# A two-layer hybrid trunk on one core: earlier input loads, a stacked low-rank product, a variance in column groups, and three probability tiles

## The chip, the cores and the metric

The kernel runs on one core of one Trainium2 chip. The metric is the time of one execution in microseconds (us): the median of three runs before the change is 1816.46 us (1814.5 to 1818.36). TensorE (PE in the profile), VectorE (DVE), ScalarE (ACT) and GpSimd (POOL) each work through a queue of their own in order; SyncE (SP) only issues transfers, and ScalarE issues a few more.

## The reference

Input x has 1024 tokens of 1024 channels. Each of two layers does:

```
h    = rms_norm(x, g_pre);  proj = h @ w_in        # split among four mixers
NSA attention | chunked gMLP | Conformer convolution | RWKV-7 recurrence
x    = x + rms_norm(concat(branch * silu(gate)) @ w_out, g_post)
x    = x + sigmoid(x @ ple_gate) * (p[layer] @ ple_proj)
```

Four pieces matter here. RWKV needs two low-rank products per token, `tanh(wd) @ w_up` for the decay and `ad @ a_up` for the gate, each with 32 inputs and 256 outputs. The convolution branch ends in a layer norm over its 256 channels, so it needs one variance per token. Attention makes, per 128 queries, head and branch (selected blocks and window), a row of softmax probabilities over up to 1024 keys. And the embedding product `p @ ple_proj` needs nothing but p, which is an input.

## The kernel before, in words

The tokens are cut in two halves of 512 per layer; layer l and half h give four rounds. Data lie channel by token (128 channels by 512 tokens). A dense product in near-float32 precision is three passes of TensorE (L166, L167, L168) over high and low parts in the type float32r: high by high, high by low, low by high. `split_w` loads 128x512 weights into `ws`, ScalarE casts the high part to `wh` (L156), GpSimd subtracts to get the low part `wl` (L158), and in the first half of a layer the low part is stored for the second. Each product of plain float32, as those with `lu`, appears in the trace as two matmul instructions.

Each round runs steps in the order that a letter string in `ORDER` gives; the first round before is "XieHFBRNrGabscdnAAATCy". X loads eight tiles of x (tag `ab`), i loads p (two tiles of tag `ld`) and splits it into four tiles of tag `t2`, e is the embedding product (48 matmuls, written to memory as `ped`), H is the norm (squares summed into `qa`, L292 to L296; column sums on TensorE, L263; then scaling, L301, and splitting, L255 and L256, into `aT`). F is the front of RWKV: the projection of low-rank inputs and gates (LO), then for each of two channel pairs the projections of k, r and v, with the two low-rank products between (L387, L392). B (`setup_late`) writes zeros to the memory tables `Xd` that RWKV's solve (R) fills in part, and builds the attention's bias tables T and TC through a gather from memory (L131) and three products (L124, L135, L141). N is the attention's front, r the recurrence, G, T and C the convolution, A one attention tile of 128 queries, a, b, c, d the gates, s the gMLP.

The strings don't fix the order of instructions. A planner orders each engine's queue at build time: every instruction has its place in the program as priority, `high_priority(offset=n)` moves one ahead by n places, and whatever is ready in the planner's own simulated time goes first by priority. On the chip a queue is in order, so an instruction that the planner took for ready holds up what stands behind it. A tag has a fixed number of tiles (`BUFS`): `t2` has 7, `r4` (probabilities, and scratch of B) has 4, `ld` 5, the score banks `s` 2, the banks `mm` 2 and `c1` 1.

Pair j of F holds the `t2` tiles k, kk, sg, aa, cum and G at once, beside the low-rank inputs `lo`, which live until the last product of pair 1.

Of the kernel before, what the change touches and what calls it, by code (L numbers as in the profile page):

```python
# [8 lines left out]
F32 = mybir.dt.float32  # L9
F32R = mybir.dt.float32r  # L10
# [6 lines left out]
TH = 512  # L17
NT = 4
# [10 lines left out]
C_ID, C_MA, C_ML, C_SUM, C_FAR, C_HB, C_FLAG, C_HS, C_N = 0, 128, 320, 384, 416, 544, 672, 673, 675  # L29
S_ANTI, S_OH, S_N = 0, 128, 256  # L30
RROW = 2128
ORDER = ("XieHFBRNrGabscdnAAATCy",
         "HAFRNGrbsaAAAAdcniOexTgCy",
         "HFRNrGabscdniOxeAAgAATyC",
         "HFRNGraAbsAAnAcdOTxgCy")
# [6 lines left out]
class Trunk:  # L42
    def __init__(self, ctx, tc, a):
# [8 lines left out]
        self.low, self.keep = {}, True  # L52
        self.setup()

    BUFS = {"aT": 16, "ws": 3, "wh": 3, "wl": 3, "t2": 7, "y": 7, "rv": 2, "pt": 3, "r4": 4, "ab": 8,
            "smr": 6, "sma": 14, "smc": 8, "cv": 4, "ot": 3, "ld": 5, "qa": 1}
    PBUFS = {"mm": 2, "s": 2, "rp": 1, "pt": 1, "pv": 1, "c1": 1}

    def t(self, shape, tag, bufs=None, dt=F32):
        self.n += 1  # L60
        return self.sb.tile(shape, dt, tag=tag, bufs=bufs or self.BUFS[tag], name=f"{tag}_{self.n}")

# [40 lines left out]
        self.mix_dram = [self.dram.tile([D, TH], F32, name=f"mixd{i}") for i in range(2)]  # L103
        self.pe_dram = [self.dram.tile([D, TH], F32, name=f"ped{i}") for i in range(2)]

    def setup_late(self):
        nc, a = self.nc, self.a
        zz = self.t([128, 1024], "r4")
        nc.vector.memset(zz, 0.0)
        for i in range(2):  # L110
            for q in range(2):
                nc.sync.dma_start(self.Xd[i][:, q * 1024:q * 1024 + 1024], zz)

        rs = self.dram.tile([4, RROW], F32, name="rscratch")
        st = self.t([128, S_N], "r4")
        nc.sync.dma_start(st[:, :S_N], a["cst"][:, C_N:C_N + S_N])
        rb = self.const([32, 4], "rb")
        nc.sync.dma_start(rb, a["rel_bias"])
        row = self.t([128, 1024], "r4")
        row2 = self.t([128, 1024], "r4")  # L120
        nc.vector.memset(row[:4, :977], 0.0)
        nc.vector.memset(row2[:4, :1023], NEG)
        pr = self.ps("pt")
        nc.tensor.matmul(pr[:4, :128], rb, st[:32, S_OH:S_OH + 128], start=True, stop=True)  # L124
        mid = self.t([128, TH], "ld")[:4, :128]
        nc.vector.tensor_copy(mid, pr[:4, :128])
        nc.sync.dma_start(rs[:, :977], row[:4, :977])
        nc.sync.dma_start(rs[:, 977:1105], mid)
        nc.sync.dma_start(rs[:, 1105:2128], row2[:4, :1023])
        hk = self.t([128, 4, 257], "r4")  # L130
        nc.sync.dma_start(hk, bass.AP(tensor=rs.tensor, offset=rs.offset + 848,  # L131
                                      ap=[[1, 128], [RROW, 4], [1, 257]]))
        for p in range(2):
            pj = self.ps("pt")
            nc.tensor.matmul(pj, st[:, S_ANTI:S_ANTI + 128],  # L135
                             hk[:, 2 * p:2 * p + 2, 1:257], start=True, stop=True)
            nc.scalar.copy(self.T[:, 2 * p:2 * p + 2, :].rearrange("p a b -> p (a b)"), pj)
        nc.vector.memset(self.TC[:, :, :53], 0.0)
        nc.vector.memset(self.TC[:, :, 70:], NEG)
        pj = self.ps("pt")  # L140
        nc.tensor.matmul(pj[:, :68], st[:, S_ANTI:S_ANTI + 128], hk[:, :, 0:257:16], start=True, stop=True)  # L141
        nc.vector.tensor_copy(self.TC[:, :, 53:70], pj[:, :68].rearrange("p (a b) -> p a b", a=4))
# [165 lines left out]
    def layer_setup(self, l):  # L308
        nc, a = self.nc, self.a
        self.l = l  # L310
        par = self.par = self.t([128, P_N], "par", bufs=2)
        nc.sync.dma_start(par, a["par"][l])
        d = self.der = self.t([128, 16], "der", bufs=2)
        nc.vector.tensor_scalar(d[:, 0:7], par[:, P_MU:P_MU + 7], -1.0, 1.0, op0=OP.mult, op1=OP.add)
        nc.vector.tensor_scalar(d[:, 7:9], par[:, P_W0:P_W0 + 2], 0.5, None, op0=OP.mult)
        nc.vector.tensor_scalar(d[:, 9:11], par[:, P_A0:P_A0 + 2], 0.5, None, op0=OP.mult)
        nc.vector.tensor_scalar(d[:, 11:13], par[:, P_KA:P_KA + 2], -1.0, 1.0, op0=OP.mult, op1=OP.add)
        cw = self.cw = self.t([128, 72], "cw", bufs=2)
        nc.vector.tensor_scalar(cw[:, :62], par[:, P_CW:P_CW + 62], 0.5, None, op0=OP.mult)
        nc.vector.tensor_scalar(cw[:, 62:66], par[:, P_CLG:P_CLG + 4], 0.5, None, op0=OP.mult)  # L320
        nc.vector.tensor_scalar(cw[:, 66:70], par[:, P_CLG:P_CLG + 4], 0.25, None, op0=OP.mult)
        nc.vector.tensor_scalar(cw[:, 70:72], par[:, P_PWB:P_PWB + 2], 0.5, None, op0=OP.mult)
        lu = self.lu = self.t([64, 256], "lu", bufs=1)
        nc.sync.dma_start(lu[0:32], a["rwkv_w_up"][l])
        nc.sync.dma_start(lu[32:64], a["rwkv_a_up"][l])
        w2 = self.w2 = self.t([128, 2, 64], "w2", bufs=1)
        nc.sync.dma_start(w2, a["nsa_w2"][l].rearrange("e p d -> p e d"))
        self.halo = None
        self.xg = None
        self.KH, self.KL, self.VS = {}, {}, {}  # L330
        self.S = None
# [15 lines left out]
    def rwkv_front(self):  # L347
        nc = self.nc
        par, der = self.par, self.der
        self.halo_in = self.halo  # L350
        self.halo_out = self.halo = self.t([128, 8], "halo", bufs=2)
        lp = self.proj([(LO0, 64), (G0, 12)])
        lo = self.shift(lp, 64, 6)
        g = self.t2(TH)
        nc.scalar.copy(g[64:76], lp[64:76])
        pg = self.ps("rp")
        for t in range(NT):
            nc.tensor.transpose(pg[:, t * 12:t * 12 + 12], g[64:76, t * 128:t * 128 + 128], self.ident[64:76, 64:76])
        self.gate = self.t([128, NT, 12], "gate", bufs=2)
        gf = self.gate.rearrange("p a b -> p (a b)")  # L360
        nc.scalar.activation(gf, pg[:, :48], AF.Tanh, scale=0.5)
        nc.vector.tensor_scalar(gf, gf, 0.5, 0.5, op0=OP.mult, op1=OP.add)
        nc.scalar.activation(lo[0:32], lo[0:32], AF.Tanh)
        self.AR, self.BK, self.v, self.yT = [], [], [], []
        self.gc = self.t([128, 2, 8], "gc", bufs=2)
        for j in range(2):
            self.rwkv_pair(j, lo)

    def rwkv_pair(self, j, lo):
        nc = self.nc  # L370
        par, der = self.par, self.der
        js = slice(j * 128, j * 128 + 128)
        c3 = lambda x: x.rearrange("p (c j) -> p c j", j=64)
        k = self.shift(self.proj(K0 + j * 128), 128, 2 + j)
# [9 lines left out]
        nc.vector.tensor_scalar(rss, pss[:, :8], 1e-24, None, op0=OP.max)  # L384
        nc.vector.reciprocal(rss, rss)
        pw_ = self.ps("c1")
        nc.tensor.matmul(pw_, self.lu[0:32, js], lo[0:32], start=True, stop=True)  # L387
        sg = self.t2(TH)
        nc.scalar.activation(sg, pw_, AF.Tanh, scale=0.5, bias=der[:, 7 + j:8 + j])
        nc.vector.tensor_scalar(sg, sg, 0.5, 0.5, op0=OP.mult, op1=OP.add)  # L390
        pa = self.ps("c1")
        nc.tensor.matmul(pa, self.lu[32:64, js], lo[32:64], start=True, stop=True)  # L392
        aa = self.t2(TH)
        nc.scalar.activation(aa, pa, AF.Tanh, scale=0.5, bias=der[:, 9 + j:10 + j])
        nc.vector.tensor_scalar(aa, aa, 0.5, 0.5, op0=OP.mult, op1=OP.add)
# [17 lines left out]
        r = self.shift(self.proj(R0 + j * 128), 128, j, "y")  # L413
# [283 lines left out]
    def conv_out(self, par, cw, l, mixd, acc, z):  # L697
        nc = self.nc
        CT = "c1"
# [3 lines left out]
        pq = self.ps(CT)  # L703
        sqs = []
        for j in range(2):
# [1 line left out]
            sq = self.t([128, 544], "cv")[:, :TH]  # L707
            nc.scalar.activation(sq, acc[j], AF.Square)
            sqs.append(sq)
        for t in range(NT):  # L710
            for j in range(2):
                nc.tensor.matmul(pq[:, t:t + 1], sqs[j][:, t * 128:t * 128 + 128], self.ones[:, 0:1],
                                 start=(j == 0), stop=(j == 1))
        r = self.rstd(pq[:, :NT], NT, 1e-5, "smc")
        pr = self.ps(CT)
        for t in range(NT):
            nc.tensor.transpose(pr[:, t * 128:t * 128 + 128], r[:, t:t + 1].to_broadcast([128, 128]), self.ident)
# [333 lines left out]
    def load_split(self, src):  # L1051
        return self.split_cm(self.ld(src))

    def embed_in(self):
        nc, a, l, h = self.nc, self.a, self.l, self.h
        pT = []
        for k in range(2):
            x = self.ld(a["pT"][l, k * 128:k * 128 + 128, h * TH:h * TH + TH])
            hi, lo = self.t2(TH, F32R), self.t2(TH, F32R)
            nc.scalar.copy(hi, x)  # L1060
            nc.vector.tensor_sub(lo, x, hi.bitcast(F32))
            pT.append((hi, lo))
        return pT
# [119 lines left out]
    def run(self):  # L1183
        prev = conv = att = None
        for l in range(2):
            self.layer_setup(l)
            for h in range(2):
                self.h = h
                self.keep = h == 0
                mixd = self.mixd = self.mix_dram[h]  # L1190
                for step in ORDER[2 * l + h]:
                    if step == "A":
# [2 lines left out]
                        self.attention(att)  # L1195
                    elif step == "H":
                        self.hT = self.norm_T()
                    elif step == "B":
                        self.setup_late()
                    elif step == "F":  # L1200
# [3 lines left out]
                    elif step == "r":  # L1204
                        self.rwkv_steps()
                    elif step == "i":
                        pT = self.embed_in()
                    elif step == "e":
                        self.keep = False
                        self.embed_out(pT)  # L1210
                        self.keep = h == 0
                    elif step == "X":
                        with self.tc.high_priority():
                            self.xs = [self.load_x(k) for k in range(KT)]
                    elif step == "n":
                        self.rwkv_norm()
# [107 lines left out]
```

## Time and profile before

| | |
|---|---|
| median of three runs | 1816.46 us |
| profiled execution, its own time | 1819.83 us |
| its span | 1818.1 us |
| TensorE busy | 1687.8 us, 93% |
| VectorE / ScalarE / GpSimd busy | 66% / 44% / 22% |
| mean granted TensorE clock | 0.96 of full |
| DMA | 261 MB, 144 GB/s in the mean |

"Busy" counts the time from an instruction's start to its modelled end, so matmuls that follow one another overlap; the distance between their starts is what they cost. Idle time of TensorE before an instruction is listed with what ended it.

### The profile page before, as it was taken

What the parts mean: (1) busy time and instruction counts of PE and PEld (TensorE: products, weight loads), DVE (VectorE), ACT (ScalarE), POOL (GpSimd) and SP (SyncE); (2) the same over time, 40 slices, a digit from 0 to 9 for tenths busy, and PEclk for the clock granted to TensorE, in tenths of its full rate; (3) what the DMA queues carried; (4) which work ended last, traced back from release to release, by engine and by line L of the source; (5) the groups of instructions that cost most, each with busy time, mean ns of one, the idle gap of its engine ahead of it and who ended that gap; (6) DMA issues with size and microseconds to landing.
All of it is one profiled execution on the core that took longest, in us unless ns stands there. A gap on an engine that the chain in (4) does not pass through costs nothing. (4 is left out here: it accounts for less than half of the span.)

```text
span 1818.1 us, 29200 instructions
## 1 busy us (share of the span) xinstructions
PE 1687.8 (93%) x10068; PEld 1242.4 (68%) x10068; DVE 1208.3 (66%) x3217; ACT 797.0 (44%) x1801; POOL 402.8 (22%) x327
## 2 busy tenths in 40 slices
PE   4998899999999999988988989999999999998998
PEld 3676666667777767666666667766777777666777
DVE  3549997764988746756498971656568885464263
ACT  3432233554234655644322344545333446554453
POOL 2333333000011232223333323000000102323343
PEclk9999998899999999999998999999989999989999
DMA  8457544235854522574574455763475433114554
GB/s 263 127 154 177 157 148 119 76 95 130 214 154 128 167 93 87 171 211 116 137 179 138 141 180 175 237 177 93 124 190 152 130 99 112 43 51 140 173 167 123
DMA packets 361419, 261.19 MB, mean 144 GB/s; under 512 B 84652, under 2 KB 296624, under 8 KB 361272
## 3 DMA queue, kind: packets, MB, share of 16 engines
q1 hardware_dynamic: 318520, 245.17, 46.6%
q10 hardware_dynamic: 42752, 14.16, 3.1%
q8 instruction: 79, 1.29, 0.3%
q14 instruction: 68, 0.56, 0.1%
HBM read 191.50 MB, written 67.77 MB: 143 GB/s over the span
## 5 line engine op out<-in xcount | busy, mean ns | idle before, releaser
L166 PE MATMUL mm<-aT,wh 128*128 128x512 f32 (+1 forms) x1304 | 536.1, 413 | 6.1 <-DVE t L742 2.0
L167 PE MATMUL mm<-aT,wh 128*128 128x512 f32 (+1 forms) x1304 | 531.3, 408 | 3.9 <-DVE aT L256 3.9
L168 PE MATMUL mm<-aT,wl 128*128 128x512 f32 (+1 forms) x1304 | 530.2, 407 | 0.2 <-POOL wl L158 0.2
L158 POOL TENSOR_TENSOR wl<-ws,wh 128x512 fp32r<-128x512 f32 (+1 forms) x228 | 308.8, 1356 | 704.3 <-ACT wh L156 596.5
L156 ACT CAST wh<-ws 128x512 fp32r<-128x512 f32 (+2 forms) x388 | 236.9, 611 | 484.7 <-PE mm L167 301.6
L166 PEld LDWEIGHTS mm<-aT,wh 128*128 128x128 f32 (+1 forms) x1304 | 249.6, 192 | 66.7 <-issue 6.0
L167 PEld LDWEIGHTS mm<-aT,wh 128*128 128x128 f32 (+1 forms) x1304 | 249.4, 191 | 58.5 <-DVE aT L256 7.6
L168 PEld LDWEIGHTS mm<-aT,wl 128*128 128x128 f32 (+1 forms) x1304 | 249.3, 191 | 51.7 <-issue 3.8
L692 DVE SCALAR_TENSOR_TENSOR cv<-cv,cw,cv 128x512 f32<-128x512 f32 x240 | 200.3, 850 | 2.3
L1030 ACT ACTIVATE r<-s,sma 128x512 f32<-128x512 f32 (+3 forms) x192 | 105.7, 554 | 51.3 <-DVE sma L1028 48.0
L606 POOL TENSOR_TENSOR q<-SB,gc 128x256 f32<-128x256 f32 x28 | 22.7, 811 | 476.3 <-DVE SB L619 178.8
L971 ACT COPY pt<-pt 128x512 f32<-128x512 f32 (+1 forms) x152 | 80.5, 530 | 104.2 <-PE pt L968 103.5
L968 PE MATMUL pt<-cst,r 128*128 128x128 f32 x528 | 103.3, 294 | 7.4 <-DVE r L1035 7.2
L976 PEld LDWEIGHTS pv<-pt,vs 128*64 128x64 f32 x1056 | 56.6, 138 | 59.3 <-ACT pt L971 47.3
L976 PE MATMUL pv<-pt,vs 128*64 128x128 f32 x1056 | 95.1, 292 | 1.7 <-ACT pt L971 1.0
L968 PEld LDWEIGHTS pt<-cst,r 128*128 128x128 f32 x528 | 60.9, 143 | 45.5 <-issue 26.7
L1020 DVE CUSTOM_DVE_ANT_0 s<-s,T 128x256 f32<-128x256 f32 (+1 forms) x144 | 54.1, 379 | 44.5 <-PE s L1001 43.5
L1000 PE MATMUL s<-kv,qs 128*128 128x512 f32 (+2 forms) x192 | 74.5, 390 | 2.0 <-ACT r L1030 1.9
L1035 DVE TENSOR_SCALAR r<-r,sma 128x640 f32<-128x640 f32 (+7 forms) x128 | 68.1, 532 | 1.0
L1001 PE MATMUL s<-kv,qs 128*128 128x512 f32 (+2 forms) x192 | 65.8, 347 | 0.0
L1032 DVE TENSOR_TENSOR sma<-sma 128x1 f32<-128x1 f32 x64 | 14.8, 231 | 71.3 <-ACT r L1030 71.0
L1110 DVE SCALAR_TENSOR_TENSOR ot<-ot,ld 128x512 f32<-128x512 f32 x24 | 25.1, 1048 | 50.3 <-ACT ot L1109 45.3
(328 smaller groups left out, 2666.5 us busy)
## 6 DMA issues: line engine op xcount, KB each, us to landing
ws<-in_w_in_dram SPq DMA_DIRECT2D x232, 256.0 KB, 3.2
wl<-low SPq DMA_DIRECT2D x156, 256.0 KB, 2.8
low<-wl SPq DMA_DIRECT2D x140, 256.0 KB, 2.1
ws<-in_ple_gate_dram SPq DMA_DIRECT2D x64, 256.0 KB, 3.1
ws<-in_w_out_dram SPq DMA_DIRECT2D x60, 256.0 KB, 2.9
ped<-ot ACTq DMA_DIRECT2D x32, 256.0 KB, 3.8
ld<-in_nsa_w_dram SPq DMA_DIRECT2D x32, 256.0 KB, 4.1
ld<-ped SPq DMA_DIRECT2D x32, 256.0 KB, 4.0
```

Of the source, the lines that this page charges most:

```text
L156: nc.scalar.copy(hi[:, :cols], st[:, :cols])
L158: nc.gpsimd.tensor_sub(lo[:, :cols], st[:, :cols], hi[:, :cols].bitcast(F32))
L166: nc.tensor.matmul(out, lh, rh, start=first, stop=False, skip_group_check=shared)
L167: nc.tensor.matmul(out, lh, rl, start=False, stop=False, skip_group_check=shared)
L168: nc.tensor.matmul(out, ll, rh, start=False, stop=last, skip_group_check=shared)
L692: nc.vector.scalar_tensor_tensor(ac, xg[j][:, k:k + TH], cw[:, j * 31 + k:j * 31 + k + 1], ac, op0=OP.mult, op1=OP.add)
L968: nc.tensor.transpose(pt[:, o:o + 128], P[e][:, (b + x - b0) * 128:(b + x - b0) * 128 + 128], self.ident)
L971: nc.scalar.copy(PT[:, :n], pt[:, :n])
L976: nc.tensor.matmul(acc[e], w.VS[hh][:, tt, br], PT[:, o:o + 128], start=False, stop=br == 1 and b + x == i, skip_group_check=True)
L1000: nc.tensor.matmul(p[:, :n], w.QS[hd][:, qs], w.KH[br, hh][:, c0 * 128:c1 * 128], start=True, stop=False)
L1030: nc.scalar.activation(P[:, o:o + wd], p[:, c:c + wd], AF.Exp, bias=ng[:, 0:1], accum_out=den[:, x:x + 1])
L1035: nc.vector.tensor_scalar(P[:, :n], P[:, :n], r, None, op0=OP.mult)
```

## The change

The first transfers: X and, in the first round, the two loads of p get an offset of 20000, ahead of the weights' 4000. `setup_late` is cut in two: the zeros for `Xd` become a step Z at its old place, and the rest (B) goes behind the gate a. The low-rank weights become one 128-row stack: high parts in rows 0 to 63, low parts in rows 64 to 127, for both products side by side; the inputs become two stacks LW and LA, so that one float32r pass of 128 rows gives what two float32 instructions over 32 rows gave. The convolution's variance has the ones as the stationary operand, four groups of 32 columns, and a transpose back. `r4` has three tiles.

```diff
-ORDER = ("XieHFBRNrGabscdnAAATCy",
+ORDER = ("XieHFZRNrGaBbscdnAAATCy",
-    BUFS = {... "r4": 4, ...}
+    BUFS = {... "r4": 3, ...}
+    def zero_tables(self):      # step Z: the memset of zz and the four stores to Xd, out of setup_late
...
-        lu = self.lu = self.t([64, 256], "lu", bufs=1)
-        nc.sync.dma_start(lu[0:32], a["rwkv_w_up"][l])
-        nc.sync.dma_start(lu[32:64], a["rwkv_a_up"][l])
+        st = self.t([128, TH], "ld")
+        for i, nm in enumerate(("rwkv_w_up", "rwkv_a_up")):
+            for r in range(4):
+                nc.sync.dma_start(st[32 * r:32 * r + 32, i * 256:i * 256 + 256], a[nm][l])
+        lu = self.lu = self.t([128, TH], "lu", bufs=1, dt=F32R)
+        nc.scalar.copy(lu, st)
+        nc.vector.tensor_sub(lu[64:128], st[64:128], lu[64:128].bitcast(F32))
...
+        LW, LA = self.t2(TH, F32R), self.t2(TH, F32R)
+        for x, hi, lw in ((LW, slice(0, 32), slice(32, 64)), (LA, slice(32, 64), slice(0, 32))):
+            nc.scalar.copy(x[hi], lo[hi])
+            nc.vector.tensor_sub(x[lw], lo[hi], x[hi].bitcast(F32))
+            nc.scalar.copy(x[64:128], x[0:64].bitcast(F32))
...
-        nc.tensor.matmul(pw_, self.lu[0:32, js], lo[0:32], start=True, stop=True)
+        nc.tensor.matmul(pw_, self.lu[:, js], LW, start=True, stop=True)
-        nc.tensor.matmul(pa, self.lu[32:64, js], lo[32:64], start=True, stop=True)
+        nc.tensor.matmul(pa, self.lu[:, 256 + j * 128:384 + j * 128], LA, start=True, stop=True)
...
-        for t in range(NT):
-            for j in range(2):
-                nc.tensor.matmul(pq[:, t:t + 1], sqs[j][:, t * 128:t * 128 + 128], self.ones[:, 0:1],
+        for j in range(2):
+            for t in range(NT):
+                nc.tensor.matmul(pq[32 * t:32 * t + 32, 0:128], self.ones[:, 0:32], sqs[j][:, t * 128:t * 128 + 128],
                                  start=(j == 0), stop=(j == 1))
-        r = self.rstd(pq[:, :NT], NT, 1e-5, "smc")
+        vr = self.t([128, 544], "cv")[:, :128]
+        nc.scalar.copy(vr, pq[:, 0:128])
+        pq = self.ps(CT)
+        nc.tensor.transpose(pq[:, 0:128], vr, self.ident)
+        r = self.rstd(pq[:, 0:128].rearrange("p (t i) -> p t i", t=NT)[:, :, 0], NT, 1e-5, "smc")
...
-    def embed_in(self):
+    def embed_in(self, first=0):
-            x = self.ld(a["pT"][l, k * 128:k * 128 + 128, h * TH:h * TH + TH])
+            with self.tc.high_priority(offset=first):
+                x = self.ld(a["pT"][l, k * 128:k * 128 + 128, h * TH:h * TH + TH])
-                        pT = self.embed_in()
+                        pT = self.embed_in(20000 if l + h == 0 else 0)
-                        with self.tc.high_priority():
+                        with self.tc.high_priority(offset=20000):
```

## Rows read from the trace of the kernel before

**Rows 1.** Page, part 1: engine, busy us, share, instructions.
```profile
PE 1687.8 (93%) x10068; PEld 1242.4 (68%) x10068; DVE 1208.3 (66%) x3217; ACT 797.0 (44%) x1801; POOL 402.8 (22%) x327
```

**Rows 2.** Waits of PE: line, releaser, total us, times, longest us.
```profile
PE mm L166 <- ACT t L1060: 18.9, 1, 18.9
...
PE pt L135 <- DMA r<-rscratch: 6.2, 1, 6.2
```

**Rows 3.** Windows: length, busy us of PE, PEld, DVE, ACT, POOL, clock, DMA, GB/s.
```profile
9.00:15.00 6.00, 0.00 (x0) 0.00 (x0) 0.00 (x0) 0.00 (x0) 0.00 (x0) 1.00 1.04 286
...
18.87:33.60 14.73, 14.73 (x53) 11.18 (x53) 8.57 (x20) 9.88 (x19) 3.75 (x3) 1.00 0.84 293
33.60:43.70 10.10, 2.50 (x14) 1.66 (x14) 4.77 (x8) 2.75 (x5) 2.25 (x2) 0.74 0.95 226
...
58.80:99.90 41.10, 39.77 (x190) 28.33 (x188) 26.33 (x56) 18.65 (x32) 16.42 (x11) 1.00 0.48 140
150.00:300.00 150.00, 133.04 (x936) 98.22 (x935) 138.95 (x318) 50.68 (x121) 53.75 (x43) 0.94 0.54 152
```

**Rows 4.** Timeline of the start: start us, us, engine, line, operation, count [idle before].
```profile
3.67 0.62 ACT L156 CAST wh<-ws 128x512 fp32r<-128x512 f32 x1 [1.59 <-DMA ws<-in_ple_proj_dram]
...
13.88 0.43 SPq L324 DMA_DIRECT2D lu<-in_rwkv_w_up_dram  x1
...
15.28 0.94 SPq L1048 DMA_DIRECT2D ld<-in_pT_dram  x2
...
18.20 0.62 ACT L1060 CAST t<-ld 128x512 fp32r<-128x512 f32 x1 [9.95 <-DMA ld<-in_pT_dram]
...
19.75 2.88 ACT L295 ACTIVATE t<-ab 128x512 f32<-128x512 f32 x5
```

**Rows 5.** Timeline of the norm's pace and of TensorE behind it.
```profile
39.01 0.68 DVE L256 TENSOR_TENSOR aT<-ab,aT 128x512 fp32r<-128x512 f32 x1
39.61 0.75 DVE L301 SCALAR_TENSOR_TENSOR ab<-ab,par,qa 128x512 f32<-128x512 f32 x1
...
42.61 2.07 PE L135 MATMUL pt<-r,r 128*128 128x512 f32 x2 [6.25 <-DMA r<-rscratch]
```

**Rows 6.** Timeline of PE around the decay's product of pair 1.
```profile
82.08 0.39 PE L167 MATMUL mm<-aT,wh 128*128 128x512 f32 x1
82.31 0.39 PE L168 MATMUL mm<-aT,wl 128*128 128x512 f32 x1
82.63 1.12 PE L387 MATMUL c<-t,lu 32*128 32x512 f32 x2
83.68 0.50 PE L166 MATMUL mm<-aT,wh 128*128 128x512 f32 x1
```

**Rows 7.** Timeline of DVE in F: pair 0's tile G, then pair 1's k.
```profile
66.25 0.07 DVE L399 MEMSET t<- 128x8 f32 x1
...
75.22 0.74 DVE L423 SCALAR_TENSOR_TENSOR y<-y,par,t 128x512 f32<-128x512 f32 x1
...
83.79 0.75 DVE L339 SCALAR_TENSOR_TENSOR t<-mm,par,t 128x511 f32<-128x511 f32 x1 [5.81 <-ACT t L338]
```

**Rows 8.** Timeline of PE: products in four column groups, and a convolution variance.
```profile
138.89 1.30 PE L869 MATMUL pt<-ld,t 128*32 128x128 f32 x40
...
1610.36 2.11 PE L712 MATMUL c<-ones,cv 128*128 128x1 f32 x16
1612.34 0.88 PE L968 MATMUL pt<-cst,r 128*128 128x128 f32 x3
```

**Rows 9.** Timeline: exponentials, and transposes that read the tile three before.
```profile
371.81 0.44 PE L968 MATMUL pt<-cst,r 128*128 128x128 f32 x2
371.90 0.57 ACT L1030 ACTIVATE r<-s,sma 128x384 f32<-128x384 f32 x1
...
1631.68 0.37 ACT L1030 ACTIVATE r<-s,sma 128x128 f32<-128x128 f32 x1 [0.17 <-DVE sma L1028]
...
1632.34 0.66 PE L968 MATMUL pt<-cst,r 128*128 128x128 f32 x4
```

More of the change, by code (lines that the diff above doesn't have):

```diff
@@ L53, in __init__ @@
         self.setup()
-    BUFS = {"aT": 16, "ws": 3, "wh": 3, "wl": 3, "t2": 7, "y": 7, "rv": 2, "pt": 3, "r4": 4, "ab": 8,
+    BUFS = {"aT": 16, "ws": 3, "wh": 3, "wl": 3, "t2": 7, "y": 7, "rv": 2, "pt": 3, "r4": 3, "ab": 8,
             "smr": 6, "sma": 14, "smc": 8, "cv": 4, "ot": 3, "ld": 5, "qa": 1}
@@ L104, in setup @@
         self.pe_dram = [self.dram.tile([D, TH], F32, name=f"ped{i}") for i in range(2)]
-    def setup_late(self):
-        nc, a = self.nc, self.a
+    def zero_tables(self):
+        nc = self.nc
         zz = self.t([128, 1024], "r4")
@@ L112, in setup_late @@
                 nc.sync.dma_start(self.Xd[i][:, q * 1024:q * 1024 + 1024], zz)
+    def setup_late(self):
+        nc, a = self.nc, self.a
         rs = self.dram.tile([4, RROW], F32, name="rscratch")
@@ L366, in rwkv_front, with rwkv_pair @@
         for j in range(2):
-            self.rwkv_pair(j, lo)
-    def rwkv_pair(self, j, lo):
+            self.rwkv_pair(j, LW, LA)
+    def rwkv_pair(self, j, LW, LA):
         nc = self.nc
@@ L1197, in run @@
                         self.hT = self.norm_T()
+                    elif step == "Z":
+                        self.zero_tables()
                     elif step == "B":
```

## The prediction

> **What bounds the kernel now.** I read the page's busy shares first, then what TensorE waited for, then the stretches, then the order of the first 60 us. TensorE is busy for 1687.8 us, 93% of the span [rows 1], so a saving counts where it takes work from TensorE while that is the engine others wait for, or removes one of its few long waits. The list of waits shows where those are: of some 130 us idle (span less busy time), one piece of 18.9 us is the start, before the first product, and one of 6.2 us is the wait of L135 for the gathered bias table [rows 2]. In the stretches the reader is to see three kinds of time. From 18.87 to 33.6 TensorE does the embedding product e without a gap; from 33.6 to 43.7 it does 2.5 us of work in 10.1 us at a clock of 0.74; in F, from 58.8 to 99.9, it is busy for 39.8 of 41.1 us [rows 3]. And from 150 to 300 VectorE is busy for 139 of 150 us, TensorE for 133: there VectorE and the recurrence's chain set the pace [rows 3].
>
> **The start.** Before, the two p loads are issued at 15.28, behind weights, constants, parameters and all of x, and the first cast of p runs at 18.20 [rows 4]. ScalarE has done one square of x by then; the next five come at 19.75, only after p's split has taken its `t2` tiles, which suggests that a tag's tiles go out in program order [rows 4]. After the change x and p are issued first, then weights. Ahead of the first product lie ten loads and one of weights, 11 x 256 KB = 2.88 MB; at the 286 GB/s of the saturated start [rows 3] that is 10.1 us. The first load of before, issued at 0.81 us, could be cast at 3.67 [rows 4], of which its own 0.9 us are in the sum, so some 2 us come on top of 0.8: p and weights are there at 12.9, and after a cast of 0.62 TensorE starts at 13.5 instead of 18.87, 5.4 earlier. If program order of the tag `ld` forced the eight small low-rank loads ahead of p, 8 x 0.43 of issue [rows 4] would take 3.4 of this back.
>
> The embedding product then runs from 13.5 to 28.2 (14.7 us, as now). Behind it, the norm: now TensorE starts F's products 10.1 us after e ended. 6.2 of these are L135, which stands ahead of F in TensorE's queue; the first `aT` pair was complete at 39.69 [rows 5], 6.1 us after e. With B gone from here F starts at 28.2 + 6.1 = 34.3. VectorE makes a pair in 0.75 + 0.69 = 1.44 us [rows 5], eight pairs end 10.1 us after the first, and the last pair's six products take 1.4: the first 48 products of F end at 45.8, where they end at 58.8 now. That is 13.0 us. Upper bound: with x there at 11 us the norm runs beside e and F starts right behind it; 48 x 0.23 [rows 6] from 28.2 end at 39.2, 19.6 us gained. Lower bound: 13.0 - 3.4 = 9.6. I take 13.0, since squares and casts stand in ScalarE's queue beside e's evacuations now as well.
>
> **B moved.** L135's first pair (2.07 us at the low clock, now in idle time [rows 5]) moves between dense work: half of it, 1.0, at full clock, and some 0.4 for the small products of L124, so +1.4. SP is passed by B's six transfers, which stood among the first weights. The wait for the gather can return: 0 to 6.2. It has dense work of a and b around it, so I take 0. Z keeps four stores of 512 KB, 7 us at 286 GB/s, beside F, which has DMA at a share of 0.48 [rows 3]: nothing; without that cover up to 3 us in weights.
>
> **The low-rank products.** The decay's product of pair 1 starts 0.32 us after the dense pass before it, where passes follow at 0.23, and the next dense pass 1.05 later [rows 6]. One float32r pass costs 0.23 in its place: at least 1.05 - 0.23 = 0.82 each, with the entry 0.91; 16 of them give 13 to 14.6 us of TensorE time. Added per round: four ScalarE copies and two subtractions of up to 0.62 and 0.69 (4 x 0.62 + 2 x 0.69 = 3.9 us), beside the dense products of k. What of the 13 us is a gain? LW and LA are two tiles of the seven where `lo` was one. Pair 0 with both is eight tiles, so its G must wait until LW is free, that is for pair 1's decay product. TensorE takes it by priority after r, v and k of dense work: now G comes at 66.25 and that product at 82.63 [rows 6, 7]. So pair 0's chain (66.25 to 75.96 [rows 7]) shifts to about 83 less what F got shorter, and pair 1's k, evacuated at 83.79 now [rows 7], waits for a tile of it. I put F's chain at the same end as now, with TensorE some 4 us ahead of it. Rounds 1 and 3 (the first halves), which VectorE and the chain pace [rows 3], then gain nothing from the product and pay two subtractions, +1.4 each; the other two keep 2 x 3.4 = 6.8. Bounds: 14.6 gained in all; or a loss, a rival below. The layer's `lu` split (one copy, one subtraction, twice) and six more issues of 0.43 on SP lie under other loads.
>
> **The variance.** 16 instructions take 1.98 us now [rows 8]; in four column groups 40 take 1.30, so 16 take 0.52 [rows 8], and the transpose 0.3, a third of 0.88: 1.2 us less of TensorE, four times. But the chain gets longer by a copy, under the 0.62 of a 512-column cast [rows 4], and the transpose, 0.9 at most. Bounds -4.8 to +3.6; I take -1.5, nearer to the TensorE row, as convolutions run beside attention.
>
> By the Trainium skill, "TensorEngine Tiling (Array Packing)", Key Properties, changing the tiling mode drains TensorE. The trace agrees with 0.32 - 0.23 = 0.09 us at the entry to the 32-row product [rows 6]. By this rule the new groups pay 2 x 0.09 four times, 0.7, and sixteen entries of 32-row products vanish, 1.4; without the rule both are zero. It changes the sum by less than a microsecond.
>
> **Three probability tiles.** I paired each of the 128 branches' exponentials with the transposes that read the tile three branches before, since with three tiles the one must wait for the other. In 12 of the 128 the exponential starts before these transposes end, first at 371.90 (end 372.1 by the modelled ends), last at 1631.68, while transposes of 1632.34 still read [rows 9]; these overlaps add up to 12.9 us. The other 116 already keep three tiles' distance, as the two banks `s` are the closer limit. What queues behind a late exponential is ScalarE's next copy `pt`, and TensorE's transposes; dense passes stand between. Bounds 0 to 13; I take 3.
>
> **Sum**, against the profiled execution's own 1819.83 us: -13.0 + 1.4 - 6.8 + 2.8 - 1.5 + 3 = -14.1, so 1805.7. The median lies 3.4 us under that execution (1816.46), so the prediction is 1802. Its own range, with half of the open bounds either way, is 1793 to 1811.
>
> **Rivals.**
> Fuller gain: the norm runs beside e (-19.6) and TensorE's saved passes count nearly in full (-11), B +1.4, variance -3, tiles +1: -31; halfway between that and the forecast, 1793. For it: TensorE at 93%. Against: ScalarE's order at the start. Chance 0.18.
> Lost on the way: the start gives 9.6, B's gather costs 3 of its 6.2, low-rank products 3, and the +1.4, +2.8 and +3 stay: -2.4, 1814. For it: the VectorE-bound stretches and a planner that doesn't know real landings. Chance 0.11.
> Three tiles bind: all 12.9 instead of 3, in attention where TensorE has idle waits for softmax: -4.2, 1812. Chance 0.08.
> The other side, the eighth `t2` tile: if the pair chains run one behind the other, F's chain ends 9.7 us later in each of four rounds, 39 us, and nothing of the 6.8 stays. With the start this is -13.0 + 1.4 + 39 + 2.8 - 1.5 + 3 = +32 at worst; with TensorE filling two of the four rounds, about +12: 1828. It decides once TensorE is idle for over 6 us per round beside F and the solve behind it. For it: the count of tiles. Against: dense work of N that is ready there. Chance 0.09.
> Transfers that don't lead: if p stays behind, the start gains only what B leaves, 6 us: 1809, within the forecast's range. Chance 0.05. The forecast itself has 0.49.
>
> **Numbers.** 0.2%, 3.6 us, is about what can be told from no change. Faster takes the forecast (0.48), the fuller gain (0.18), the transfers that don't lead (0.05) and half the third, 0.75; slower the eighth tile and a piece of the second, 0.13; same 0.12. The range 1785 to 1818 leaves out the eighth tile and the far ends.
>
> **What would show it.** Right: the first L166 near 13.5, F's first 48 products ended near 46, no wait of L135 before F; L387 and L392 at 0.23 each; G of pair 0 behind pair 1's L387; four quick groups in L712's place; ScalarE waits for L968 a little more often. Wrong: a first product later than 17, TensorE idle beside F or before L538, the gather's wait back at 6 us, or attention tiles over 1 us longer each.

## The result, and the profile after: 1.35% slower

The changed kernel takes 1841.55 us in the median of four runs (1836.29 to 1841.92), the kernel before beside it 1815.49: a ratio of 1.0135, interval 1.0117 to 1.0152. The forecast was 1802, with 1785 to 1818 as its range. The profiled execution has a span of 1839.5 us (own time 1841.4), 21.4 more than before. Lines are shifted: the dense passes are L168, L169 and L170, the low-rank products L398 and L403, G's memset L410, the column groups of attention L884.

The page's first part, columns as in [rows 1]:

```profile
PE 1682.2 (91%) x10056; PEld 1236.3 (67%) x10056; DVE 1212.2 (66%) x3227; ACT 810.3 (44%) x1823; POOL 393.8 (21%) x327
```

TensorE has less to do than before (1682.2 for 1687.8) and the span is longer: its idle time has grown by 27 us, to 157. The list of TensorE's waits (line, releaser, total, times, longest) answers [rows 2]; the last line is of the kernel before, where the column groups are L869:

```profile
PE pt L884 <- DMA ld<-in_nsa_w_dram: 33.5, 12, 9.7
PE mm L168 <- ACT t L1076: 20.7, 1, 20.7
...
PE mm L265 <- DVE qa L298: 4.9, 1, 4.9
...
PE pt L869 <- DMA ld<-in_nsa_w_dram: 15.9, 9, 4.3
```

The start has grown from 18.9 to 20.7, L135's wait is gone and L265's stands in its place, and the attention's column groups wait 33.5 us for weights (15.9 before). The windows answer [rows 3], for the embedding product, the norm, F, and 150 to 300 with its first third:

```profile
20.66:35.40 14.74, 14.06 (x48) 10.58 (x48) 6.12 (x9) 9.70 (x18) 2.99 (x3) 1.00 0.82 285
35.40:46.00 10.60, 2.88 (x12) 2.39 (x13) 3.34 (x6) 2.85 (x6) 2.29 (x2) 0.71 1.00 315
59.90:109.00 49.10, 43.64 (x200) 33.64 (x200) 27.02 (x57) 21.37 (x36) 15.27 (x12) 0.90 0.45 131
...
150.00:300.00 150.00, 129.59 (x910) 93.99 (x909) 134.16 (x317) 49.00 (x117) 45.45 (x40) 0.90 0.55 150
150.00:200.00 50.00, 34.82 (x169) 25.41 (x168) 47.17 (x91) 9.94 (x21) 15.62 (x11) 0.83 0.59 144
```

F and its products took 41.1 us and take 49.1, at a clock of 0.90 instead of 1.00. From 150 to 300 TensorE is busy for 129.6 us (133.0 before); most of the idle time lies in the first third. Why the start is late stands in the timeline of SP and ScalarE [rows 4]:

```profile
16.50 0.49 SPq L328 DMA_DIRECT2D ld<-in_rwkv_w_up_dram  x1
17.04 0.89 SPq L1063 DMA_DIRECT2D ld<-in_pT_dram  x2
17.98 1.35 SPq L328 DMA_DIRECT2D ld<-in_rwkv_w_up_dram  x3
...
19.99 0.62 ACT L1076 CAST t<-ld 128x512 fp32r<-128x512 f32 x1 [6.78 <-DMA ld<-in_pT_dram]
```

p is issued right behind the first of the low-rank staging loads, at 17.04 (15.28 before), though its offset is 20000. Both take tiles of the tag `ld`, and the staging tile comes first in the program. The norm follows the embedding product as late as before: its column sums stand at 39.66, F's products at 46.00 [rows 5].

```profile
39.66 1.76 PE L265 MATMUL mm<-onec,qa 128*128 128x1 f32 x8 [4.93 <-DVE qa L298]
...
46.00 1.13 PE L168 MATMUL mm<-aT,wh 128*76 128x512 f32 x2 [2.11 <-ACT aT L257]
```

In F, the timelines of PE [rows 6] and of DVE [rows 7]:

```profile
82.75 0.40 PE L170 MATMUL mm<-aT,wl 128*128 128x512 f32 x1
82.98 0.39 PE L398 MATMUL c<-t,lu 128*128 128x512 f32 x1
83.21 0.40 PE L168 MATMUL mm<-aT,wh 128*128 128x512 f32 x1
```

```profile
69.82 1.23 DVE L408 TENSOR_TENSOR_SCAN t<-scanm,t 128x512 f32<-128x512 bf16 x1
...
83.45 0.07 DVE L410 MEMSET t<- 128x8 f32 x1 [3.84 <-PE c L398]
...
90.80 1.75 DVE L434 SCALAR_TENSOR_TENSOR y<-y,par,t 128x512 f32<-128x512 f32 x1
```

A low-rank product costs 0.23, as dense passes do. Pair 0's decays are summed by 71 us (the scan, L408), and its G comes at 83.45, released by pair 1's L398: the eighth tile. The chain behind it ends at 92.6 instead of 75.96 [rows 7]. It is so in every round: from the start of pair 0's scan to its G the four rounds take 13.6, 26.1, 13.6 and 25.1 us, where they took 1.2 to 2.5 before, and each time G follows pair 1's L398 by 0.4 to 0.6.

### The profile page after: what moved, and what is told of

Its sections match the earlier page's. It is cut to its first block, busy times and chain, and to the rows that moved or that the text cites. A ratio compares the mean times of both kernels' runs of the same rounds, so it can differ in the third digit from the quotient of the medians.

```text
span 1839.5 us, 29256 instructions
## 1 busy us (share of the span) xinstructions
PE 1682.2 (91%) x10056; PEld 1236.3 (67%) x10056; DVE 1212.2 (66%) x3227; ACT 810.3 (44%) x1823; POOL 393.8 (21%) x327
## 3 DMA queue, kind: packets, MB, share of 16 engines
q1 hardware_dynamic: 319096, 245.57, 45.8%
## 5 line engine op out<-in xcount | busy, mean ns | idle before, releaser
L168 PE MATMUL mm<-aT,wh 128*128 128x512 f32 (+1 forms) x1304 | 540.9, 417 | 11.8 <-DVE y L668 4.2
L169 PE MATMUL mm<-aT,wh 128*128 128x512 f32 (+1 forms) x1304 | 533.5, 410 | 3.6 <-DVE aT L258 3.5
L170 PE MATMUL mm<-aT,wl 128*128 128x512 f32 (+1 forms) x1304 | 532.9, 409 | 0.0
L160 POOL TENSOR_TENSOR wl<-ws,wh 128x512 fp32r<-128x512 f32 (+1 forms) x228 | 301.5, 1325 | 699.1 <-ACT wh L158 590.4
L168 PEld LDWEIGHTS mm<-aT,wh 128*128 128x128 f32 (+1 forms) x1304 | 250.8, 193 | 74.4 <-ACT aT L257 6.9
L169 PEld LDWEIGHTS mm<-aT,wh 128*128 128x128 f32 (+1 forms) x1304 | 250.8, 192 | 58.2 <-DVE aT L258 7.5
L170 PEld LDWEIGHTS mm<-aT,wl 128*128 128x128 f32 (+1 forms) x1304 | 250.3, 192 | 52.5 <-issue 2.5
L703 DVE SCALAR_TENSOR_TENSOR cv<-cv,cw,cv 128x512 f32<-128x512 f32 x240 | 195.8, 835 | 2.2
L617 POOL TENSOR_TENSOR q<-SB,gc 128x256 f32<-128x256 f32 x28 | 21.4, 763 | 499.4 <-DVE SB L630 206.2
L258 DVE TENSOR_TENSOR aT<-ab,aT 128x512 fp32r<-128x512 f32 x64 | 51.0, 801 | 6.4 <-ACT aT L257 6.1
```

Of the source, the lines that this page charges most:

```text
L160: nc.gpsimd.tensor_sub(lo[:, :cols], st[:, :cols], hi[:, :cols].bitcast(F32))
L168: nc.tensor.matmul(out, lh, rh, start=first, stop=False, skip_group_check=shared)
L169: nc.tensor.matmul(out, lh, rl, start=False, stop=False, skip_group_check=shared)
L170: nc.tensor.matmul(out, ll, rh, start=False, stop=last, skip_group_check=shared)
L703: nc.vector.scalar_tensor_tensor(ac, xg[j][:, k:k + TH], cw[:, j * 31 + k:j * 31 + k + 1], ac, op0=OP.mult, op1=OP.add)
```

## The experiments

Each was timed beside the kernel before, whose medians in the four groups of kernels were 1816.0 to 1816.8 (1747 to 1749 at full clock). A kernel has four or ten timed runs, and they spread by 4 to 22 us; the interval is that of the ratio, so two medians that differ by a few us are often not clear of noise. A second number helps to read them: the span times its mean granted clock, in the median of all timed runs of a kernel, is what TensorE's clock offered, in microseconds at 2.4 GHz ("at full clock" below). The rest of the span is what the 1.2 GHz level left out. It is a split and not a price, for a stretch that waits on another engine at the low level loses nothing by it.

| kernel | median us | ratio to before, interval | at full clock | left out |
|---|---|---|---|---|
| before (beside the last group, 31 runs) | 1816.5 | | 1747 | 67 |
| after | 1841.6 | 1.0135 [1.0117, 1.0152] | 1759 | 81 |
| no_stack | 1803.1 | 0.9919 [0.9888, 0.995] | 1740 | 60 |
| stack_only | 1845.4 | 1.0153 [1.0118, 1.0189] | 1756 | 88 |
| t2_eight | 1811.9 | 0.998 [0.9959, 1.0] | 1742 | 68 |
| decay_early | 1811.4 | 0.9972 [0.9952, 0.9992] | 1747 | 63 |
| stage_in_pt | 1825.5 | 1.0045 [1.0025, 1.0064] | 1754 | 69 |
| eight_and_pt | 1806.8 | 0.9941 [0.992, 0.9962] | 1732 | 73 |
| eight_no_stack | 1810.3 | 0.9974 [0.9954, 0.9994] | 1746 | 62 |
| no_stack_eight | 1800.0 | 0.9922 [0.9895, 0.9948] | 1742 | 55 |
| one_pass | 1802.4 | 0.9927 [0.9903, 0.9951] | 1736 | 65 |
| three_p_tiles | 1814.7 | 0.9985 [0.9969, 1.0002] | 1746 | 68 |
| start_only | 1809.2 | 0.9961 [0.9942, 0.9979] | 1740 | 69 |
| variance_only | 1829.4 | 1.0065 [1.0042, 1.0088] | 1753 | 73 |
| start_three | 1806.6 | 0.9941 [0.992, 0.9961] | 1741 | 63 |
| mended_old_variance | 1820.2 | 1.0031 [1.0005, 1.0057] | 1733 | 86 |
| variance_three | 1823.2 | 1.0028 [1.0004, 1.0053] | 1753 | 68 |
| variance_moved | 1813.2 | 0.9986 [0.9962, 1.0009] | 1749 | 62 |

### Which part costs it

**no_stack**: the change without the stack.

```diff
-        lu = self.lu = self.t([128, TH], "lu", bufs=1, dt=F32R)     # and st, LW, LA and their copies
+        lu = self.lu = self.t([64, 256], "lu", bufs=1)
-        nc.tensor.matmul(pw_, self.lu[:, js], LW, start=True, stop=True)
+        nc.tensor.matmul(pw_, self.lu[0:32, js], lo[0:32], start=True, stop=True)
```

> The changed kernel without the stacked low-rank product: lu, its two loads and the four-pass products as before; early loads, moved tables, column-group variance and three probability tiles stay. If the stack is the whole loss (by the tile it needs and by its staging tile ahead of p): 1803 to 1810, as then the start's gain of 10 us is left. If the other three edits cost time as well: 1815 or more.

**stack_only**: the kernel before with the stack and with three probability tiles.

```diff
-    "r4": 4
+    "r4": 3
-        nc.tensor.matmul(pw_, self.lu[0:32, js], lo[0:32], start=True, stop=True)
+        nc.tensor.matmul(pw_, self.lu[:, js], LW, start=True, stop=True)     # with st, lu, LW and LA as in the change
```

> The kernel before with the stacked low-rank product and three probability tiles alone (with four there is no room for the stack's tiles). If the stack is the loss: 1835 to 1845, F's chain ends about 10 us later in every round. If the loss comes of the moved tables or the variance: within 5 us of 1816.

The stack is the whole loss: without it 1803.1, 38.5 under the change; with nothing else but the three tiles 1845.4, 29 over before (three tiles alone cost nothing, see below). All the rest of the change together gains 14. The two figures for the stack need not be equal: in the change its staging tile also holds p up, which the section on the start prices.

### What in the stack costs it

**t2_eight** gives the change one more tile of the tag.

```diff
-    "t2": 7
+    "t2": 8
```

> The changed kernel with eight t2 tiles in place of seven, nothing else. Theory 1 (the eighth tile: pair 0's G waits for pair 1's decay product, each round's F chain ends about 10 us later): G of pair 0 comes within 5 us of its scan again, F's chain ends some 9 us earlier in each round, and the time falls by 20 us or more, to 1821 or less. Rival (the loss is the start, where p's loads were held behind the low-rank staging tile): this changes nothing at the start, the time stays within 5 us of 1841.

**decay_early** keeps seven tiles and moves one product: pair 1's L398 goes ahead, so that LW is read for the last time before pair 0 wants its G.

```diff
-        pw_ = self.ps("c1")
-        nc.tensor.matmul(pw_, self.lu[:, js], LW, start=True, stop=True)
+        with self.tc.high_priority(offset=1000 * j):
+            pw_ = self.ps("c1")
+            nc.tensor.matmul(pw_, self.lu[:, js], LW, start=True, stop=True)
```

> The changed kernel, seven t2 tiles, with pair 1's decay product moved ahead by 1000 places in priority, so that it runs as soon as pair 0's gate product has left its bank c1; LW is then free before pair 0's G wants a tile. Theory 1 in its narrow form (it is the wait of G for that one product): G of pair 0 comes within 3 us of its scan in all rounds and the time falls like with eight tiles, to 1808 to 1818. Rival (seven tiles are too few for the rest of F and N whatever the order): the time stays over 1830.

Two different edits, one that gives the tile and one that frees it earlier, take 30 us off alike (1811.9, 1811.4). So the wait for the tile cost these 30 us, and neither the copies nor the product's form, which both edits keep. In both, pair 0's G comes within 2.3 us of the start of its scan in all four rounds. The timelines of decay_early, PE and then DVE (its lines are one higher):

```profile
66.68 0.50 PE L399 MATMUL c<-t,lu 128*128 128x512 f32 x1
...
71.50 0.49 PE L399 MATMUL c<-t,lu 128*128 128x512 f32 x1
```

```profile
72.07 0.07 DVE L411 MEMSET t<- 128x8 f32 x1
```

Both products now stand within 5 us, and G follows the second by 0.6. The first round's solve begins (L456) at 112.9 there and at 117.0 in t2_eight, at 121.0 after the change; the difference between the change and t2_eight is 4.0, 20.5, 27.7 and 35.9 us where the solve of each of the four rounds begins, 33.5 at the end. A part of it is F itself, and a part comes later: in the change the attention's weights (`nsa_w`) reach TensorE late.

```profile
168.38 0.66 PE L884 MATMUL pt<-ld,t 128*32 128x128 f32 x8 [9.71 <-DMA ld<-in_nsa_w_dram]
```

```profile
153.27 0.55 SPq L485 DMA_DIRECT2D l<-Nd  x1
...
162.41 0.33 SPq L163 DMA_DIRECT2D low<-wl  x1
...
163.67 1.06 SPq L844 DMA_DIRECT2D ld<-in_nsa_w_dram  x2
```

SP issues these loads at 163.67, 18 us after the first of the column groups (145.59). Ahead of them in its queue stand the solve's last transfer (153.27) and two more turns of weights, the second of which waits for GpSimd's low part until 162.41. In t2_eight the first of them goes right behind the solve's last transfer, at 151.14, 4.0 us behind its first group, as it did before (142.92 and 138.89). So some 3 us of this come from a later solve, and the rest from the order in which the planner queued SP's transfers. The wait for them in t2_eight, and in no_stack with its first product:

```profile
PE pt L884 <- DMA ld<-in_nsa_w_dram: 15.6, 9, 4.2
```

```profile
PE pt L875 <- DMA ld<-in_nsa_w_dram: 15.4, 9, 5.0
PE mm L168 <- ACT wh L158: 13.2, 1, 13.2
```

It is 34.4 in stack_only and 16.1 in decay_early: the wait comes and goes with the tile. Why the planner put the loads further back where the tile was short was not looked into.

### The start

**stage_in_pt** takes the staging tile from another tag.

```diff
-        st = self.t([128, TH], "ld")
+        st = self.t([128, TH], "pt")
```

> The changed kernel with the low-rank staging tile in the tag pt in place of ld, so that p's two loads really go out right behind x. The start theory: first product near 13.5 us in place of 20.7, the norm's column sums some 7 us earlier, and 7 to 10 us off the time (1832 to 1834). Theory 1 alone: the start gains those microseconds and the eighth tile still costs its 25, so 1832 as well or a little less; if the gain is swallowed by the recurrence's chain, 1838 to 1841.

```profile
PE pt L884 <- DMA ld<-in_nsa_w_dram: 34.3, 12, 9.7
PE mm L168 <- ACT wh L158: 13.4, 1, 13.4
```

With nothing else changed p leads, the first product starts at 13.4 and F's products at 34.16 (46.00 after the change): the tag's order was what held p. That is 11.8 us at F, and 16.0 in the median, more than the 7 to 10 expected; where the other 4 arise is not shown. The late weights stay, so they belong to the eighth tile and not to the start.

**eight_and_pt** has both repairs, `"t2": 8` and the tag "pt".

> The changed kernel with both: eight t2 tiles, and the staging tile in pt so that p's loads lead. If the two losses are separate and add up (some 29 us and 16 us off 1841.5): 1796 to 1800. If the start's gain is part of what the eight tiles give back: 1805 to 1812.

1806.8, 34.7 under the change where the two gave 29.7 and 16.0 alone: they overlap.

**start_only** is the kernel before with only this part.

```diff
-ORDER = ("XieHFBRNrGabscdnAAATCy",
+ORDER = ("XieHFZRNrGaBbscdnAAATCy",
-                        with self.tc.high_priority():
+                        with self.tc.high_priority(offset=20000):     # and p's loads, as in the change
```

> The kernel before with the early loads and the moved tables alone (four probability tiles, variance as before). Worked out ahead: first product near 13.5, F's first 48 products ended near 46, 10 to 13 us gained, so 1803 to 1806. If the variance or the three tiles had a part in the 1803 of the kernel without the stack: 1808 or more.

The first product starts at 13.16, F's at 34.25, and the first 48 of F end at 49.3: 9.7 us earlier than before. Where the first solve begins 3.3 of these are left, at the first product that reads `Xd` (L538 in the kernel before) 1.7. The median is 7 lower, but the profiled execution is the slowest of its ten (1818.9), so it can't show where those 7 arise. L137, the product of the moved bias table, waits 1.5 for its gather. By its expectation 1808 or more means that the other edits have a part in the 1803.1 of no_stack; with three tiles added (start_three, below) it is 1806.6, and the step from there to 1803.1 is not clear of noise.

### What the saved TensorE time is worth

**eight_no_stack**: the kernel before with `"t2": 8` and `"r4": 3`. **no_stack_eight**: no_stack with `"t2": 8`.

> Control: the kernel before with eight t2 tiles and three probability tiles, no other edit. If eight tiles are a gain by themselves, this is faster than before by 5 us or more and the fall seen with eight tiles in the changed kernel is not all the wait of G. If the tile only pays what LW and LA cost: 1813 to 1820.

> Early loads, moved tables, column groups and three probability tiles without the stack, with eight t2 tiles. Eight tiles alone gave about 6 us on the kernel before: if that adds up, 1797; if the eighth tile only reshuffles, 1801 to 1806. This is the version that should beat both kernels.

**one_pass** is no_stack with the low-rank product as one float32r pass over rounded inputs and weights; the low parts are left out of the computation.

```diff
-        nc.sync.dma_start(lu[0:32], a["rwkv_w_up"][l])
-        nc.sync.dma_start(lu[32:64], a["rwkv_a_up"][l])
+        lu = self.lu = self.t([64, 256], "lu", bufs=1, dt=F32R)
+        nc.scalar.copy(lu, st)
...
+        lr = self.t2(TH, F32R)
+        nc.scalar.copy(lr[0:64], lo[0:64])
```

> The changed kernel without the stack, but with the low-rank products as one float32r pass of 32 rows on rounded inputs; the low parts of inputs and weights are left out. It takes the stack's saving of TensorE time (16 x 0.85 us = 13 us) with one ScalarE copy and one short-lived tile a round and no subtraction. If TensorE's time in F is worth its length: 1803 less 7 to 13, so 1790 to 1796. If F's chain and VectorE set the pace, so that the stack had nothing to gain even with a tile to spare: 1800 to 1806.

The tile is worth something by itself: on the kernel before, eight_no_stack takes 5.7 us off (0.9974, the interval ends at 0.9994), which by its expectation means that not all of t2_eight's 30 is the wait of G. decay_early takes off as much with seven tiles, so the wait alone can account for them. In no_stack_eight the tile gives 3 us, between the two values expected and within the noise.

With eight tiles, the stack (eight_and_pt) takes 1806.8 and no stack (no_stack_eight) 1800.0; the intervals of their ratios overlap, so no gain of the stack is seen, and no sure loss. At full clock it is 1732 us for 1742, and 18 more are left out by the clock. A reading that fits, and that no window here was taken to show, is that TensorE has less to do in stretches that other engines pace, and falls to the low level in some of them. one_pass, which saves without the two tiles and the subtractions (its low-rank products are busy for 10.7 us less than no_stack's), ends within a microsecond of no_stack. The two intervals leave some 7 us open either way, so a TensorE saving of some 11 us beside F has shown no gain here, and is not worth its length.

### Three probability tiles

**three_p_tiles**: the kernel before with `"r4": 3` alone.

> The kernel before with three probability tiles in place of four. Worked out ahead of the result: 3 us more (0 to 13), so 1817 to 1822. If attention is bound by the tiles: 1825 or more.

ScalarE's waits in this kernel, exponentials behind transposes:

```profile
ACT r L1030 <- PE pt L968: 16.4, 12, 2.9
```

Before there was one such wait, of 2.9 us. The other eleven, 13.5 us together, are close to the bound that the prediction counted (12 exponentials, 12.9 us), and they cost nothing that shows: 1814.7 to 1816.0.

### The variance

**variance_only**: the kernel before with the variance's lines of the change.

```diff
-                nc.tensor.matmul(pq[:, t:t + 1], sqs[j][:, t * 128:t * 128 + 128], self.ones[:, 0:1],
+                nc.tensor.matmul(pq[32 * t:32 * t + 32, 0:128], self.ones[:, 0:32], sqs[j][:, t * 128:t * 128 + 128],
+        vr = self.t([128, 544], "cv")[:, :128]
+        nc.scalar.copy(vr, pq[:, 0:128])
+        nc.tensor.transpose(pq[:, 0:128], vr, self.ident)
```

> The kernel before with the column-group variance alone. TensorE spends 1.2 us less on each of four, the chain gets up to 0.9 longer: 1812 to 1817. If the change of tiling mode or the longer chain costs: 1819 or more.

It cost 13 us where -1.5 was forecast, with -4.8 to +3.6 as bounds. Its profile shows where: at 457, in the second round and past the first round's variance (310), it stands 0.9 us ahead of before. At 579 the recurrence's products are 6 us behind and the dense passes beside them 14 to 16, and at 790, where only dense passes stand, they are 15 behind. That round's own variance comes only at 741. Windows of TensorE there, and two of the same windows in the kernel before:

```profile
450.00:470.00 20.00, 18.80 (x122) 14.56 (x121) 15.95 (x49) 6.65 (x11) 0.00 (x0) 1.00 0.88 194
470.00:482.50 12.50, 11.93 (x51) 7.99 (x52) 11.26 (x27) 2.96 (x9) 1.26 (x2) 0.59 0.69 188
482.50:542.50 60.00, 58.23 (x455) 45.69 (x453) 51.48 (x124) 19.86 (x43) 4.80 (x7) 1.00 0.65 184
542.50:557.50 15.00, 13.97 (x97) 10.13 (x98) 10.58 (x29) 2.59 (x8) 1.47 (x3) 0.54 0.07 19
...
470.00:482.50 12.50, 12.50 (x65) 9.73 (x61) 11.72 (x28) 4.85 (x12) 1.26 (x2) 1.00 0.88 254
542.50:557.50 15.00, 15.00 (x124) 10.35 (x123) 12.42 (x43) 7.29 (x22) 1.05 (x1) 1.00 0.39 111
```

and what TensorE did ahead of the first fall:

```profile
470.57 0.43 PE L873 MATMUL pt<-ld,t 128*32 128x128 f32 x8 [1.77 <-DMA ld<-in_nsa_w_dram]
```

In the trace of before the granted clock is 1.00 in each of these four stretches, with a longest wait of 1.18 us (468.27). Here it falls after the wait of 1.77, and again at 542.5 behind waits of 0.56 and 0.63. The two low stretches leave out 12.5 x 0.41 + 15 x 0.46 = 12.0 us, while TensorE is busy for 93 to 95% of them. TensorE's queue is also in another order there: between 457 and 579 dense passes and the recurrence's products have changed places. Is that the variance's doing? Four more kernels ask.

**start_three** is no_stack with the old variance; **mended_old_variance** is eight_and_pt with it; **variance_three** is variance_only with `"r4": 3`.

> The kernel before with the early loads, the cut into Z and B, and three probability tiles: the change without the stack and with the old variance. Theory A, the new variance's longer chain (copy and transpose) costs the 13 us that it cost alone: this runs 13 us under the same kernel with the new variance (1803), at 1790. Theory B, those 13 us are the planner's new order of TensorE's queue, and above all stretches at the 1.2 GHz level behind short waits (79.9 us of clock lost in that profile against 70.3 before), not the variance's own work: 1799 to 1807, within 4 us of 1803.

> The change with eight t2 tiles and the staging tile out of the loads' tag, and the old variance. Theory A: 13 us under the same with the new variance (1806.8), 1794. Theory B: within 5 us of it, 1802 to 1812; the clock lost in the profile tells on which side.

> The kernel before with the new variance and three probability tiles. Three tiles alone gave -1.3. Theory A: 1828, the sum of the two. Theory B: the order is another again, so the 13 us need not come back: 1812 to 1826, with the loss of clock following the time.

**variance_moved** is the kernel before with its old products in another place of the queue.

```diff
-        for t in range(NT):
-            for j in range(2):
+        with self.tc.high_priority(offset=100):
+            for t in range(NT):
+                for j in range(2):
```

> The kernel before with the old variance's sixteen products 100 places earlier in the planner's priority, and no instruction added or taken away. Theory A (only added work costs): 1816 within 3 us. Theory B (the order decides): the time moves by over 4 us one way or the other, and the span less the clock lost in it moves by less than that.

Theory A falls. The same edit costs 13.3 on before and 8.5 beside three tiles, gains 3.5 in start_three's company (1806.6 to 1803.1, within the noise) and gains 13.4 in the mended version (1820.2 to 1806.8). At full clock (before 1748 beside variance_only) these are +4, +7, -1 and -1; the part left out by the clock is +6, 0, -3 and -13 (medians, whose parts need not add up to the whole). So the edit has no price of its own of 13 us: without the low level it is between -1 and +7 us by the version, and the largest figure, of the mended version, is all clock. That a new order of TensorE's queue brings these about is argued and not shown. Theory B's bounds held start_three and variance_three, the latter without the loss of clock that it named; mended_old_variance ended 8 us outside them, by its clock. In variance_moved the time moved by 3.3 us, not over 4, and the interval takes in no change: that one decides nothing. What makes one order keep the clock and another lose it was not settled.

## Why the prediction was wrong, step by step

- **The low-rank products, the step that failed: "I put F's chain at the same end as now."** Forecast -6.8 + 2.8 = -4.0; measured +38.5 with all else in place (no_stack to after) and +31 on three_p_tiles; the wait for the tile is 30 of the 38.5 (t2_eight, decay_early). The pieces were right: 0.23 for each product, so that L387 and L392 went from 18.5 us busy to 7.1; G of pair 0 at 83.45, where "about 83" was forecast. Wrong was what followed from it. Pair 0's chain did shift in every round, TensorE did not fill the hole, and the attention's weights came late in SP's queue. This is the rival "the eighth `t2` tile", which had 0.09. The 30 us lie between its 19 for two rounds and its 39 for four; that no_stack to after comes to 38.5 is chance, for p's late start is in that figure, the rounds lose unequal amounts (4.0, 16.5, 7.2 and 8.2 us from solve to solve, by the differences above), and the late weights were not in the rival. I halved it with the argument that dense work of N was ready. The windows above speak against that: 43.6 busy of 49.1 us at a clock of 0.90, where F before had 39.8 of 41.1 at full clock.
- **The start.** Forecast -13.0, first product at 13.5; measured in the change 20.66, and F's first 48 products end at 59.96, where 45.8 was forecast and the kernel before has 58.99. The rows said that a tag's tiles go out in program order, and the prediction named the staging loads as a risk of 3.4 us. It priced the eight issues only. p stood behind the first of them, which is issued after weights, constants and parameters, so the first product came 7 us later than forecast. With p free the steps were right: 13.4 and 34.16 in stage_in_pt for 13.5 and 34.3. The forecast end of the 48, 45.8 for 49.3 to 49.8, was 3.5 to 4 us too early: it took VectorE's pace of 1.44 us a pair, 11.5 us for all, and the stretch takes 15.0 to 15.6 at a mean clock of 0.80 to 0.81, as it did before (15.3 at 0.84). Of the 9.7 us gained there 7 reach the end (start_only, B's move included, where the two terms gave -11.6).
- **B moved.** No wait of L135 before F, right; its products moved to about 209 us, with a wait of 1.5 in start_only and none in the change. Not measured by itself.
- **The variance.** In the trace of after the sixteen instructions take 0.64 us and not 0.52; the next dense pass stands 0.81 behind the first of them, 0.17 of it its own wait for ScalarE:

```profile
752.51 0.40 PE L170 MATMUL mm<-t,wl 128*128 128x512 f32 x1
752.84 0.64 PE L723 MATMUL c<-cv,ones 128*32 128x128 f32 x16
753.65 0.50 PE L168 MATMUL mm<-t,wh 128*128 128x512 f32 x1 [0.17 <-ACT ot L1085]
```

  So these instructions were priced nearly right, and the time still went by -13 to +13 us with the version; the term had no place in a sum made to a microsecond. The first group starts 0.33 after the dense pass, where passes follow at 0.23, and the 128-row L398 starts at 0.23. That agrees with the drain at a change of the tiling mode that the Trainium skill names ("TensorEngine Tiling (Array Packing)", Key Properties).
- **Three probability tiles.** Forecast +3; the waits came as counted, the time did not (-1.3 us, the interval 0.9969 to 1.0002).
- **The numbers.** "Slower" had 0.13. The two large steps both failed through the stack, one by its tiles of `t2` and one by its staging tile of `ld`, so that their failures came together; the cases were weighed as if they were apart.

## What to carry to other kernels

Count tiles per tag at the moment of most need, and treat one too many as a wait for the last reader of the earliest tile: price it by that reader's place in its queue, and don't discount it for work that could fill the hole unless the trace shows that work there. Test it twice, by a tile more and by an earlier last reader, as a tile can be a gain by itself. Under this planner a load with the highest priority still waits for the tiles of its tag that the program takes earlier, so a load that must lead needs a tag in which nothing stands ahead of it. Before a saving on a 93% busy engine is booked, ask who paces the stretch that it comes from.

## What the runs showed of the hardware that was not expected

Two versions that agree within a microsecond and a half at full clock (eight_and_pt and mended_old_variance, 1732 and 1733) differ by 13 us in time, all of it in what the low level left out. In variance_only a wait of 1.77 us ahead of 470.57 was followed by a granted clock of 0.59 in the window to 482.5, one of 1.18 in the trace of before by none below 1.00; but the second fall, at 542.5, came behind waits of 0.56 and 0.63, so the longest wait alone does not tell. Over the eighteen kernels the medians of what the low level left out run from 55 to 88 us, and three versions that differ by under 11 us at full clock (mended_old_variance 1733, eight_and_pt 1732, no_stack_eight 1742) come out as 1820, 1807 and 1800, in the order of what the low level left out (86, 73 and 55); the last two are not clear of noise from each other. The record of the clock seems blind at the very start: the embedding product's first passes stand 0.43 us apart (22.41, 22.84, 23.27 after the change), where they follow at 0.23 later, while the granted clock of its window reads 1.00.
